# GELU as tanh inside the state-space units of a Hymba-style block, with the mixing stage reading its result directly

## The chip, the cores and the metric

The kernel runs on one core of a Trainium2 chip. The metric is the device time of one execution in microseconds (us). The core has a matrix engine (TensorE, PE; its weight loads are listed apart as PEld), an elementwise engine (VectorE, DVE), an engine for functions and copies (ScalarE, ACT), a slower general engine (GpSimd, POOL) and a queue engine that issues most DMAs (SyncE, SP). Each engine runs its own instructions in order; between engines they wait on semaphores.

## The reference

One layer of a streaming encoder, sequence 2048, model width 1024, all in float32. A normalised input is projected into two head groups. Group A is a state-space layer (32 channel groups of 16, a diagonal complex state of 64 per group), group B chunked attention (8 heads of 64, 64-frame chunks, 8 chunks back, relative-position bias). Both outputs are normalised, joined, projected and added to the input, and a SwiGLU feed-forward follows. The part that the change touches:

```python
def s5_mixer(u, ..., d_skip, w_glu, b_glu):
    ...
    _, states = lax.associative_scan(combine, (a, bu), axis=1)
    y = jnp.einsum('bsgp,ghp->bsgh', states, c_mat).real + d_skip * uf
    y = jax.nn.gelu(y.reshape(bsz, seq, D_SSM))
    y = y * jax.nn.sigmoid(y @ w_glu + b_glu)
    return y
```

`jax.nn.gelu` is here the tanh form, 0.5 y (1 + tanh(sqrt(2/pi) (y + 0.044715 y^3))).

## The kernel before

Matrix products that need float32 accuracy are made from three float32r products: an operand is split into a high part (a cast on ACT) and a low part (a subtraction on DVE). `split` (L151) does both, and `mm3` (L145) the three products.

Time runs in four stages. Up to about 130 us the input of the state-space layer is projected and its matrices are prepared. Then comes **attention** with 128 steps (4 blocks of 512 positions, 8 heads, 4 query tiles of 128 each), up to about 725 us. After it the **mixing stage** (normalisation, sigmoid gate, output projection), up to about 970 us, and the feed-forward.

In an attention step `s` the loop at the end of `att_phase` puts out, in this order of ORDER = "sptf": the scores of step `s` (`sc`, PE; the biased minimum `mn`, DVE; `exp`, ACT, L865), the transposes of step `s - 2` (`pt`, PE, L877; the cast `pth`, ACT, L880; the difference `ptl`, DVE, L881), products with V every four steps (`pj`; `yt` on ACT, `ya` on DVE), and filler. The banks `sc` and `pt` exist once, `pj` twice. PE's instructions keep the order of the program (`Ordered`, PINA), the other engines' instructions are placed by a scheduler, in an order that is then fixed.

Filler is a list of `Unit`s. Each is a generator with a number of pieces, a first step `s0` and an end step `s1`; its first piece may come `pre` steps earlier. Projections of later blocks (`hT_unit`, `qk_unit`, `v_unit`) are units, and so is the state-space layer: eight batches `b` of four channel groups, each with a front and a back.

- `ssm_front(b)` loads `U` (the input, for even `b` from 2 on in the space of `rsn`) and the input matrices, multiplies (`pj`), copies the result to `X` (ACT, L578), and runs the scan over `X` on POOL (L592 to L604). POOL then sends `X`, shifted by one, by four DMAs into `XG` (L626). `X`, `XG` and the odd `U` exist once.
- `ssm_back(b)` loads its two matrices, and in two halves `q` multiplies `U` and `XG` into `pj` and copies it back over `U` (ACT, L648). Eight DMAs on SP store `U` as `y` (L651).

The fronts begin at the steps in SX and last 9 steps, the backs begin at those in SY and last 2.

`mix_phase` works on the four blocks of 512 positions. `fetch` (L1030) loads `y` for two blocks into the tile `yr`, in the order j, c of the state-space layer (position = 8 c + j). `load` applies GELU on ACT, in blocks 0 and 1 by one instruction of 128x2048, in 2 and 3 by four of 128x512, and writes `ys` in order of position; then it splits `ys` into `gh`, `gl`. `load_a` loads the attention outputs `ya` and squares and sums them (`squares`). `glu` multiplies `gh`, `gl` by the gate matrix, adds the bias, takes the sigmoid and multiplies `ys` by it. In blocks 0 and 1 (`late`) the four biased products are put down in `yr`, and one sigmoid of 128x2048 follows; in 2 and 3 each product has its own sigmoid into `sg`. Sums of squares go through PE and a chain of 15 small DVE instructions (`newton`, ending in `no`). The first pieces of `mix_phase`, up to the gates of blocks 0 and 1, are laid into the last attention steps, from step OPEN = 119 on, and the load of the gate matrix (`wgh`, `wgl`, through two buffers `sg`) with them.

Of the kernel before, what the change touches and what calls it, by code (L numbers as in the profile page):

```python
# [16 lines left out]
P = 128  # L17
# [5 lines left out]
L = 8  # L23
# [30 lines left out]
X1B = 6  # L54
TAIL = (0, 512), (512, 256), (768, 256)
MAGIC = 12582912.0
F2 = NF // 2
SB_, CB_, GB_ = 5, 5, 10
DG = 3
# [91 lines left out]
def split(k, hi, lo, raw):  # L151
    nc = k.nc
    return nc.scalar.copy(hi, raw), nc.vector.tensor_tensor(lo, raw, f32(hi), op=ALU.subtract)  # L153
# [400 lines left out]
def ssm_front(k, p, psum, S, b, eng):  # L554

    nc = k.nc

    def load(out, in_):
        ins = nc.sync.dma_start(out, in_)
        if b == 0:  # L560
            k.tc.keep_in_program_order(ins)

    U = S["rsn"][:, : GB * NC].rearrange("p (g c) -> p g c", g=GB) if b and b % 2 == 0 else k.t(p, "U", [P, GB, NC])[:]
    k.U[b] = U
    for j in range(L):
        load(U[j * CH : (j + 1) * CH].rearrange("c g (n t) -> c g n t", n=NSB), S["u"].rearrange("(c g) n j t -> c g n j t", c=CH)[:, GB * b : GB * b + GB, :, j])
    bst = k.t(p, "Bst", [P, GB, P])
    load(bst[:].rearrange("p g m -> p (g m)"), S["bst"][b // 2][:, (b % 2) * GB * P : (b % 2 + 1) * GB * P])
    yield

    X = k.t(p, "X", [P, 2, GP, NC])
    for q in range(GP):
        ps = k.t(psum, "pj", [P, 2, NC], bufs=2)
        for g2 in range(2):
            k.ta.matmul(ps[:, g2, :], bst[:, 2 * q + g2, :], U[:, 2 * q + g2, :], start=True, stop=True)
        for g2 in range(2):
            for c in range(2):
                nc.scalar.copy(X[g2 * NS : (g2 + 1) * NS, c, q, :], ps[c * NS : (c + 1) * NS, g2, :])  # L578
        yield

    a8 = S["a8"]
    qs = slice(GP * b, GP * b + GP)
    Xk = X[:].rearrange("p r q (k s) -> p r q k s", s=8)
    Xe = Xk[:, :, :, :, 7].rearrange("p r q (a b) -> p r q a b", b=8)

    def step(dst, src, e, n):

        ar = a8[:, 0, qs, (0, 7, 15)[e]].unsqueeze(1).to_broadcast([P, 2, GP]).unsqueeze(3).to_broadcast([P, 2, GP, n])
        aw = S["sw"][:, e, :, qs].unsqueeze(3).to_broadcast([P, 2, GP, n])
        t = k.t(p, "st1", [P, 2, GP, NC // 8])  # L590
        t2 = k.t(p, "st2", [P, 2, GP, NC // 8])
        eng.tensor_tensor(t[:, :, :, :n], src, ar, op=ALU.mult)  # L592
        eng.tensor_tensor(t2[:, :, :, :n], src[:, ::-1], aw, op=ALU.mult)
        eng.tensor_tensor(dst, dst, t[:, :, :, :n], op=ALU.add)  # L594
        eng.tensor_tensor(dst, dst, t2[:, :, :, :n], op=ALU.add)  # L595

    def carry(dst, end, i0, n):

        for c in range(2):
            for e in range(2):  # L600
                t = k.t(p, "fx", [P, GP, NC // 8, 7])[:, :, :n]
                pw = a8[:, c if e == 0 else 1 - c, qs, i0 : i0 + 7].unsqueeze(2).to_broadcast([P, GP, n, 7])
                eng.tensor_tensor(t, end[:, e].unsqueeze(3).to_broadcast([P, GP, n, 7]), pw, op=ALU.mult)  # L603
                eng.tensor_tensor(dst[:, c], dst[:, c], t, op=ALU.subtract if e == 1 and c == 0 else ALU.add)  # L604
            yield

    for s in range(1, 8):
        step(Xk[:, :, :, :, s], Xk[:, :, :, :, s - 1], 0, NC // 8)
        yield
    for b_ in range(1, 8):  # L610
        step(Xe[:, :, :, :, b_], Xe[:, :, :, :, b_ - 1], 1, 4)
        yield
    for a in range(1, 4):
        step(Xe[:, :, :, a : a + 1, 7], Xe[:, :, :, a - 1 : a, 7], 2, 1)
        yield
    yield from carry(Xe[:, :, :, 1:, :7], Xe[:, :, :, :3, 7], 8, 3)
    yield from carry(Xk[:, :, :, 1:, :7], Xk[:, :, :, : NC // 8 - 1, 7], 0, NC // 8 - 1)

    if b == 0:
        k.XG = k.t(p, "XG", [P, GB, NC])  # L620
        nc.gpsimd.memset(k.XG[:, :, 0:1], 0.0)
    XG = k.XG
    XGv = XG[:].rearrange("p (q g) c -> p q g c", g=2)
    for g2 in range(2):
        for c in range(2):
            eng.dma_start(XGv[c * NS : (c + 1) * NS, :, g2, 1:], X[g2 * NS : (g2 + 1) * NS, c, :, : NC - 1])  # L626
    yield


def ssm_back(k, p, psum, S, b):  # L630

    nc = k.nc
    F = GB * CH
    gs = slice(GB * b, GB * b + GB)
    tm = k.t(p, "Tm", [P, GB, P])
    for i in range(L):
        nc.sync.dma_start(tm[i * CH : (i + 1) * CH], S["kt"].rearrange("c g a m -> c g (a m)")[:, gs, P - CH * i : 2 * P - CH * i])
    vm = k.t(p, "Vm", [P, GB, P])
    nc.sync.dma_start(vm[:], S["v"].rearrange("q g c n m -> (c n) (q g) m")[:, gs, CH:])
    yield  # L640
    U, XG = k.U.pop(b), k.XG
    for q in range(GP):
        ps = k.t(psum, "pj", [P, 2, NC], bufs=2)
        for g2 in range(2):
            g = 2 * q + g2
            k.ta.matmul(ps[:, g2, :], tm[:, g, :], U[:, g, :], start=True, stop=False)
            k.ta.matmul(ps[:, g2, :], vm[:, g, :], XG[:, g, :], start=False, stop=True)
        nc.scalar.copy(U[:, 2 * q : 2 * q + 2, :], ps[:])  # L648
        yield
    for j in range(L):  # L650
        nc.sync.dma_start(S["y"][b * F : (b + 1) * F, j, :].rearrange("(g c) t -> c g t", c=CH), U[j * CH : (j + 1) * CH])  # L651
    yield


SSM_F = 1 + GP + 7 + 7 + 3 + 4 + 1
SSM_B = 1 + GP + 1
SX = 4, 24, 35, 48, 61, 74, 87, 100
SY = 20, 36, 49, 62, 75, 88, 101, 114


class Unit:
# [21 lines left out]
def att_phase(k, ident, S, aw, x0, roots):  # L683

    tc, nc, io, pfs = k.tc, k.nc, k.io, k.pfs
    with ExitStack() as cx:
# [263 lines left out]
        k.U = {}  # L950
        for b in range(NG // GB):
            units.append(Unit(ssm_front(k, sp, psum, S, b, k.ssm_eng), SSM_F, SX[b], SX[b] + 9, SX[b] - 2 if b == 0 else 2 if b == 1 else 5, light=SL))
            units.append(Unit(ssm_back(k, sp, psum, S, b), SSM_B, SY[b], SY[b] + 2, 6, light=SL))
        N = len(steps)
        for s in range(N + LAG + 2):
            if s == OPEN:
# [24 lines left out]
def mix_phase(k, S, bank):  # L981
# [3 lines left out]
    with ExitStack() as cx:  # L985
# [46 lines left out]
            for f in range(4):  # L1032
                nc.sync.dma_start(yrs[0][:, f], S["y"][f * P : (f + 1) * P, :, sb * 64 : sb * 64 + 128])

        def load(sb, one=False):
            b = B()
            b.o = {}
            yt = k.t(my, "ys", [P, 4, SB], bufs=2)
            b.ys, b.g = [yt[:, f] for f in range(4)], []
            if sb and sb % 2 == 0:  # L1040
                fetch(sb)
            yv = b.yr = yrs[0][:, :, :, (sb % 2) * 64 : (sb % 2 + 1) * 64]
            fs = [slice(0, 4)] if one else [slice(f, f + 1) for f in range(4)]
            for s in fs:
                nc.scalar.activation(yt[:, s].rearrange("p f (c j) -> p f c j", j=L), yv[:, s].rearrange("p f j c -> p f c j"), AF.Gelu_apprx_tanh)
            for f in range(4):
                gh, gl = k.t(my, f"gh{f}", [P, SB], F32R), k.t(my, f"gl{f}", [P, SB], F32R)
                split(k, gh[:], gl[:], b.ys[f])
                b.g.append((gh, gl))
            return b  # L1050

# [5 lines left out]

        def glu(b, bank, late=False):


            def by8(a):
                return a.rearrange("p (a b) -> p a b", a=L)

            for f in range(4):
                ps = bank()
                cs = slice(f * P, (f + 1) * P)
                for q in range(4):
                    mm3(te, ps[:, :512], Wg[q][0][:, cs], Wg[q][1][:, cs], b.g[q][0][:], b.g[q][1][:], q == 0, q == 3)
                    if q < 3:
                        yield  # L1070
                if late:
                    nc.vector.tensor_scalar(b.yr[:, f], by8(ps[:, :512]), bg[:, f : f + 1], None, op0=ALU.add)
                    if f == 3:
                        nc.scalar.activation(b.yr, b.yr, AF.Sigmoid)
                        for i in range(4):
                            nc.vector.tensor_tensor(by8(b.ys[i]), by8(b.ys[i]), b.yr[:, i], op=ALU.mult)
                else:
                    sg = k.t(mz, "sg", [P, SB], bufs=SGB)
                    nc.scalar.activation(sg[:], ps[:, :512], AF.Sigmoid, bias=bg[:, f : f + 1])
                    nc.vector.tensor_tensor(b.ys[f], b.ys[f], sg[:], op=ALU.mult)  # L1080
                yield
            b.sqs = squares(b.ys)

# [73 lines left out]
        yield  # L1157
        mw = rx.enter_context(tc.tile_pool(name="mw", reuse_waits="tile", bufs=2, side="right"))
        wr = rx.enter_context(tc.tile_pool(name="wr", reuse_waits="tile", bufs=2, side="right"))
        b = load(0, True)  # L1160
        load_a(b, 0)
        raws = [load_wo(n, wr, "xt") for n in range(2)]
        for _ in range(PY):
# [1 line left out]
        for n, _ in enumerate(glu(b, bank, True)):  # L1165
# [4 lines left out]
                spread(k, te, pb, b.o[0], 0)  # L1170
                rstd2(b, 0, pb[:])
            yield
        nxt = load(1, True)
        for _ in range(PZ):
            yield

# [551 lines left out]
```

## Time and profile before

| | us |
|---|---|
| median of 3 runs | 2274.19 |
| lowest, highest | 2266.21, 2277.7 |
| the profiled execution | 2277.4 |
| its span in the trace | 2275.6 |

Busy in that span: PE 2169.8 us, DVE 1542.7, ACT 1002.5, POOL 350.1; mean granted clock of PE 0.978. ACT has 15 loads of a function table, 1283 ns each.

A line of a group names the source line, engine, operation, output and inputs with shapes and the count; then busy us and the mean ns of one; then the engine's idle time just before these instructions and what ended it. A line of the timeline begins with the start and the duration in us; the bracket at its end is the idle time of the engine before it and what released it. A line of waits gives the engine and the tile it wrote, what it waited for, the total in us, the number of times and the longest. A line by stretches gives the stretch, its length, the busy time of PE, PEld, DVE, ACT and POOL with counts, the granted clock, and the share and rate of the DMA engines. L153 is the line in `split`, L76 and L79 are PE's products and transposes, `SPq` and `POOLq` are queues that issue DMAs.

### The profile page before, as it was taken

What the parts mean: (1) busy time and instruction counts of PE and PEld (TensorE: products, weight loads), DVE (VectorE), ACT (ScalarE), POOL (GpSimd) and SP (SyncE); (2) the same over time, 40 slices, a digit from 0 to 9 for tenths busy, and PEclk for the clock granted to TensorE, in tenths of its full rate; (3) what the DMA queues carried; (4) which work ended last, traced back from release to release, by engine and by line L of the source; (5) the groups of instructions that cost most, each with busy time, mean ns of one, the idle gap of its engine ahead of it and who ended that gap; (6) DMA issues with size and microseconds to landing.
All of it is one profiled execution on the core that took longest, in us unless ns stands there. A gap on an engine that the chain in (4) does not pass through costs nothing.

```text
span 2275.6 us, 30307 instructions
## 1 busy us (share of the span) xinstructions
PE 2169.8 (95%) x10632; PEld 1828.5 (80%) x10632; DVE 1542.7 (68%) x2695; ACT 1002.5 (44%) x1656; POOL 350.1 (15%) x827
## 2 busy tenths in 40 slices
PE   8989898999997899999999999999999999999997
PEld 6778787888986688878888887888888777888886
DVE  7757556555556756776767678666666477688776
ACT  6446555455557452343333335333333443353322
POOL 2246666646520000000000000000000010000000
PEclk9999999999998899999999999999999999999999
DMA  8778875766653535854555467655433395465652
GB/s 296 234 250 263 220 195 172 220 197 185 177 166 105 172 118 160 270 179 144 178 183 193 163 213 259 196 175 185 143 93 115 110 389 169 166 226 182 218 179 75
DMA packets 214874, 428.36 MB, mean 188 GB/s; under 512 B 38848, under 2 KB 61424, under 8 KB 207616
## 3 DMA queue, kind: packets, MB, share of 16 engines
q1 hardware_dynamic: 207072, 401.49, 54.6%
q0 software_dynamic: 7648, 24.92, 3.3%
q8 instruction: 84, 1.38, 0.2%
q14 instruction: 70, 0.57, 0.1%
HBM read 286.86 MB, written 129.00 MB: 183 GB/s over the span
## 4 chain that ended last, share of the span: by engine, by line
PE 77%; DMA 5%; DVE 5%; issue 4%; POOL 3%; ACT 2%; SPq 1%; DVEq 0%; ACTq 0%; POOLq 0%
PE X L76 20%; PE ps L76 17%; PE Y L76 10%; PE big L76 9%; PE pf L76 8%; PE W L76 5%; PE pj L76 3%; PE sc L76 2%; DMA acc<-x 2%; PE pt L79 2%; POOL X L595 1%; POOL X L594 1%; DMA lo<-hc 1%; POOL X L604 1%; POOL fx L603 1%
## 5 line engine op out<-in xcount | busy, mean ns | idle before, releaser
L76 PE MATMUL X<-hi,c 128*128 128x512 f32 x1408 | 451.3, 391 | 6.2 <-DVE c L153 5.5
L76 PE MATMUL ps<-hd,hd 128*128 128x512 f32 (+1 forms) x1968 | 429.7, 380 | 3.9 <-DVE hd L153 2.0
L76 PEld LDWEIGHTS ps<-hd,hd 128*128 128x128 f32 x1968 | 357.6, 189 | 74.6 <-DVE hd L153 2.7
L76 PEld LDWEIGHTS X<-hi,c 128*128 128x128 f32 x1408 | 265.4, 189 | 62.7 <-DVE c L153 6.4
L76 PE MATMUL X<-lo,c 128*128 128x512 f32 x704 | 274.9, 390 | 0.0
L153 ACT CAST hd<-hd 128x1536 fp32r<-128x1536 f32 (+1 forms) x106 | 147.3, 1393 | 234.6 <-DMA hd<-hq 148.1
L76 PE MATMUL Y<-hi,c 128*128 128x512 f32 x704 | 224.7, 390 | 2.1 <-DVE u L1407 2.1
L153 DVE TENSOR_TENSOR hd<-hd 128x1536 fp32r<-128x1536 f32 (+1 forms) x106 | 174.0, 1643 | 37.1 <-ACT hd L153 36.5
L153 DVE TENSOR_TENSOR c<-S,c 128x512 fp32r<-128x512 f32 x176 | 120.8, 687 | 98.9 <-ACT c L153 98.7
L1511 POOL DMA_DIRECT2D hd<-hq x7 | 5.3, 762 | 1169.5 <-PE X L76 1158.0
L1403 ACT COPY u<-X 128x512 f32<-128x512 f32 x132 | 77.3, 586 | 200.6 <-PE X L76 200.6
L76 PE MATMUL big<-m,woh 128*128 128x512 f32 x512 | 163.1, 400 | 0.0
L153 ACT CAST c<-S 128x512 fp32r<-128x512 f32 x176 | 109.3, 621 | 119.0 <-PE Y L76 61.8
L1545 DVE TENSOR_TENSOR acc<-acc,ps 128x512 f32<-128x512 f32 x196 | 130.3, 681 | 41.0 <-PE ps L76 40.7
L76 PEld LDWEIGHTS Y<-hi,c 128*128 128x128 f32 x704 | 132.3, 188 | 30.4 <-DVE u L1407 2.9
L76 PEld LDWEIGHTS X<-lo,c 128*128 128x128 f32 x704 | 132.8, 189 | 27.7
L76 PE MATMUL pf<-hi,w 128*128 128x512 f32 x416 | 150.7, 414 | 0.8 <-ACT hi L741 0.8
L153 ACT CAST c<-raw 128x512 fp32r<-128x512 f32 x132 | 82.2, 622 | 151.0 <-PE Y L76 64.3
L881 DVE TENSOR_TENSOR ptl<-pt,pth 128x640 fp32r<-128x640 f32 (+3 forms) x152 | 98.2, 646 | 66.6 <-ACT pth L880 64.8
L76 PE MATMUL Y<-lo,c 128*128 128x512 f32 x352 | 137.0, 389 | 0.0
L865 ACT ACTIVATE s<-s,mn 128x640 f32<-128x640 f32 (+4 forms) x128 | 97.9, 765 | 74.1 <-DVE mn L862 67.1
L880 ACT CAST pth<-pt 128x640 fp32r<-128x640 f32 (+3 forms) x152 | 83.6, 550 | 82.6 <-PE pt L79 77.6
(448 smaller groups left out, 4280.6 us busy)
## 6 DMA issues: line engine op xcount, KB each, us to landing
w<-wss SPq DMA_DIRECT2D x36, 1024.0 KB, 6.6
hq<-g SPq DMA_DIRECT2D x140, 256.0 KB, 2.1
hd<-hq SPq DMA_DIRECT2D x35, 768.0 KB, 4.5
hd<-wc SPq DMA_DIRECT2D x35, 768.0 KB, 5.9
raw<-in_w_gate SPq DMA_DIRECT2D x44, 512.0 KB, 3.7
raw<-in_w_up SPq DMA_DIRECT2D x44, 512.0 KB, 4.2
wc<-px SPq DMA_DIRECT2D x66, 256.0 KB, 2.9
wss<-w SPq DMA_DIRECT2D x12, 1024.0 KB, 5.8
```

Source lines behind the costliest of these rows:

```text
L76: return self.tc.keep_in_program_order(self.tc.nc.tensor.matmul(*a, **b))
L79: return self.tc.keep_in_program_order(self.tc.nc.tensor.transpose(*a, **b))
L153: return nc.scalar.copy(hi, raw), nc.vector.tensor_tensor(lo, raw, f32(hi), op=ALU.subtract)
L594: eng.tensor_tensor(dst, dst, t[:, :, :, :n], op=ALU.add)
L595: eng.tensor_tensor(dst, dst, t2[:, :, :, :n], op=ALU.add)
L603: eng.tensor_tensor(t, end[:, e].unsqueeze(3).to_broadcast([P, GP, n, 7]), pw, op=ALU.mult)
L604: eng.tensor_tensor(dst[:, c], dst[:, c], t, op=ALU.subtract if e == 1 and c == 0 else ALU.add)
L865: nc.scalar.activation(s[:, :nk], s[:, :nk], AF.Exp, bias=mn[:], scale=-1.0, accum_out=sums[sb, pr][:, hh, qp : qp + 1])
L880: nc.scalar.copy(pth[:, a:b, qp, :], pt[:, a:b, :])
L881: nc.vector.tensor_tensor(ptl[:, a:b, qp, :], pt[:, a:b, :], f32(pth[:, a:b, qp, :]), op=ALU.subtract)
L1403: nc.scalar.copy(u[:], ps[:])
L1545: V.tensor_tensor(a, a, ps[:], op=ALU.add)
```

## The change

Each half of a back now leaves 0.5 y in `U` (ACT copy with a scale), its square in the same half of `XG`, then on DVE (square + 0.25/0.044715) times 0.5 y, tanh on ACT with the remaining factor as its scale, and on DVE (tanh + 1) times 0.5 y over `U`. A back has 8 pieces in place of 4 and takes 4 steps; from the fourth batch on fronts start every 12 steps instead of 13, and from the third on backs come earlier (the last at step 108 instead of 114). Since `XG` is overwritten, POOL clears its first column for each batch. `load` no longer calls GELU: the splits read `yr` itself, its rows j in steps of 128 elements, and write `gh` and `gl` in order of position. The late sigmoid works in `ys`, and the final product multiplies the sigmoid by `yr`, again read across its rows.

```diff
     if b == 0:
         k.XG = k.t(p, "XG", [P, GB, NC])
-        nc.gpsimd.memset(k.XG[:, :, 0:1], 0.0)
     XG = k.XG
+    nc.gpsimd.memset(XG[:, :, 0:1], 0.0)
...
-        nc.scalar.copy(U[:, 2 * q : 2 * q + 2, :], ps[:])
+        u, t = U[:, 2 * q : 2 * q + 2, :], XG[:, 2 * q : 2 * q + 2, :]
+        nc.scalar.activation(u, ps[:], AF.Copy, scale=0.5)
+        nc.scalar.activation(t, u, AF.Square)
+        yield
+    for q in range(GP):
+        u, t = ...
+        nc.vector.scalar_tensor_tensor(t, t, 0.25 / GELU, u, op0=ALU.add, op1=ALU.mult)
+        nc.scalar.activation(t, t, AF.Tanh, scale=8.0 * GELU * math.sqrt(2.0 / math.pi))
+        yield
+    for q in range(GP):
+        u, t = ...
+        nc.vector.scalar_tensor_tensor(u, t, 1.0, u, op0=ALU.add, op1=ALU.mult)
         yield
...
-SSM_B = 1 + GP + 1
-SX = 4, 24, 35, 48, 61, 74, 87, 100
-SY = 20, 36, 49, 62, 75, 88, 101, 114
+SSM_B = 1 + 3 * GP + 1
+SX = 4, 24, 35, 47, 59, 71, 83, 95
+SY = 20, 36, 48, 60, 72, 84, 96, 108
...
-            units.append(Unit(ssm_back(k, sp, psum, S, b), SSM_B, SY[b], SY[b] + 2, 6, light=SL))
+            units.append(Unit(ssm_back(k, sp, psum, S, b), SSM_B, SY[b], SY[b] + 4, 6, light=SL))
...
-            for s in fs:
-                nc.scalar.activation(yt[:, s].rearrange("p f (c j) -> p f c j", j=L), yv[:, s].rearrange("p f j c -> p f c j"), AF.Gelu_apprx_tanh)
+            b.yr = yrs[0][:, :, :, (sb % 2) * 64 : (sb % 2 + 1) * 64].rearrange("p f j c -> p f c j")
             for f in range(4):
-                split(k, gh[:], gl[:], b.ys[f])
+                split(k, byt(gh[:]), byt(gl[:]), b.yr[:, f])
...
                 if late:
-                    nc.vector.tensor_scalar(b.yr[:, f], by8(ps[:, :512]), bg[:, f : f + 1], None, op0=ALU.add)
+                    nc.vector.tensor_scalar(b.ys[f], ps[:, :512], bg[:, f : f + 1], None, op0=ALU.add)
                     if f == 3:
-                        nc.scalar.activation(b.yr, b.yr, AF.Sigmoid)
+                        nc.scalar.activation(b.yt[:], b.yt[:], AF.Sigmoid)
                         for i in range(4):
-                            nc.vector.tensor_tensor(by8(b.ys[i]), by8(b.ys[i]), b.yr[:, i], op=ALU.mult)
+                            nc.vector.tensor_tensor(byt(b.ys[i]), byt(b.ys[i]), b.yr[:, i], op=ALU.mult)
                 else:
-                    nc.vector.tensor_tensor(b.ys[f], b.ys[f], sg[:], op=ALU.mult)
+                    nc.vector.tensor_tensor(byt(b.ys[f]), byt(sg[:]), b.yr[:, f], op=ALU.mult)
```

The order that each engine gets is fixed when the kernel is built. ACT near the end of attention, before, from a head's `exp` (`s`) to the casts of block 0 for the gate; `pth` is the cast of the transposes, `yt` the copy behind the products with V:

```order
L865 ACTIVATE s_8141,sm_8105<-s_8141,mn_8142 128x640
L1045 ACT_TABLE_LOAD
L1045 ACTIVATE ys_8185<-yr_8069 128x2048
L153 CAST wgh_1709_8074<-sg_8076 128x512
L153 CAST wgh_1712_8080<-sg_8082 128x512
L904 COPY yt_8166<-pj_8149 64x512
L880 CAST pth_8169<-pt_8171 128x5x128
L153 CAST gh_1741_8187<-ys_8185 128x512
L153 CAST gh_1743_8191<-ys_8185 128x512
L153 CAST gh_1745_8195<-ys_8185 128x512
L153 CAST gh_1747_8199<-ys_8185 128x512
```

The same place now (source lines are 12 higher in this part):

```order
L154 CAST gh_1741_8257<-yr_8140 128x512
L877 ACTIVATE s_8192,sm_8176<-s_8192,mn_8193 128x640
L892 CAST pth_8087<-pt_8196 128x5x128
L154 CAST gh_1743_8261<-yr_8140 128x512
L877 ACTIVATE s_8212,sm_8176<-s_8212,mn_8213 128x640
L154 CAST gh_1745_8265<-yr_8140 128x512
L154 CAST gh_1747_8269<-yr_8140 128x512
L154 CAST wgh_1709_8145<-sg_8147 128x512
L154 CAST wgh_1712_8151<-sg_8153 128x512
L916 COPY yt_8237<-pj_8220 64x512
L892 CAST pth_8240<-pt_8242 128x5x128
```

The load and the GELU are gone, and the four casts have moved ahead of the `yt` and `pth` behind which they stood. In the whole order of ACT 3 table loads are left of 15.

SP at the same place, before: loads of the gate matrix through `sg`, and of the attention outputs of block 0 (`ya_1749` to `ya_1752`):

```order
L1000 DMA sg_8082<-in_w_glu 128x512
L549 DMA nbb_1549<-nbs_69 64x576
L550 DMA nbb_1549<-nbs_69 64x576
L1055 DMA ya_1749_8203<-ya_s_66 128x512
L1055 DMA ya_1750_8204<-ya_s_66 128x512
L1055 DMA ya_1751_8205<-ya_s_66 128x512
L1055 DMA ya_1752_8206<-ya_s_66 128x512
L1000 DMA sg_8088<-in_w_glu 128x512
L1000 DMA sg_8094<-in_w_glu 128x512
```

SP now:

```order
L1012 DMA sg_8153<-in_w_glu 128x512
L550 DMA nbb_1549<-nbs_69 64x576
L551 DMA nbb_1549<-nbs_69 64x576
L1067 DMA ya_1749_8273<-ya_s_66 128x512
L1012 DMA sg_8159<-in_w_glu 128x512
L1012 DMA sg_8165<-in_w_glu 128x512
L1067 DMA ya_1750_8274<-ya_s_66 128x512
L1067 DMA ya_1751_8275<-ya_s_66 128x512
L1067 DMA ya_1752_8276<-ya_s_66 128x512
```

Three of the four `ya` loads have moved behind the second pair of loads of the gate matrix, which need the `sg` buffers free again.

DVE in the last back, now: the four three-operand products (`XG`, `U`) among the minimum of the scores (`mn`) and the `ptl` of attention; before, none of the four was there:

```order
L800 TENSOR_TENSOR k_1588_7439<-pf_7521,k_1588_7439 64x512
L655 SCALAR_TENSOR_TENSOR XG_2225<-XG_2225,U_6701 128x512
L874 ISA s_7659,mn_7660<-sc_7654,nbb_1549 128x640
L874 ISA mn_7660 128x1
L660 SCALAR_TENSOR_TENSOR U_6701<-XG_2225,U_6701 128x512
L655 SCALAR_TENSOR_TENSOR XG_2225<-XG_2225,U_6701 128x512
L893 TENSOR_TENSOR ptl_7561<-pt_7663,pth_7560 128x5x128
L660 SCALAR_TENSOR_TENSOR U_6701<-XG_2225,U_6701 128x512
```

Each `U` product stands ahead of the next softmax instruction of DVE and needs a Tanh of ACT first.

More of the change, by code (lines that the diff above doesn't have):

```diff
@@ L56 @@
 MAGIC = 12582912.0
+GELU = 0.044715
 F2 = NF // 2
@@ L647, in ssm_back @@
             k.ta.matmul(ps[:, g2, :], vm[:, g, :], XG[:, g, :], start=False, stop=True)
-        nc.scalar.copy(U[:, 2 * q : 2 * q + 2, :], ps[:])
+        u, t = U[:, 2 * q : 2 * q + 2, :], XG[:, 2 * q : 2 * q + 2, :]
[3 more added lines that the diff above has]
+    for q in range(GP):
+        u, t = U[:, 2 * q : 2 * q + 2, :], XG[:, 2 * q : 2 * q + 2, :]
+        nc.vector.scalar_tensor_tensor(t, t, 0.25 / GELU, u, op0=ALU.add, op1=ALU.mult)
+        nc.scalar.activation(t, t, AF.Tanh, scale=8.0 * GELU * math.sqrt(2.0 / math.pi))
+        yield
+    for q in range(GP):
+        u, t = U[:, 2 * q : 2 * q + 2, :], XG[:, 2 * q : 2 * q + 2, :]
+        nc.vector.scalar_tensor_tensor(u, t, 1.0, u, op0=ALU.add, op1=ALU.mult)
         yield
@@ L1033, in fetch, with byt, load @@
                 nc.sync.dma_start(yrs[0][:, f], S["y"][f * P : (f + 1) * P, :, sb * 64 : sb * 64 + 128])
-        def load(sb, one=False):
+        def byt(a):
+            return a.rearrange("p (c j) -> p c j", j=L)
+        def load(sb):
             b = B()
             b.o = {}
-            yt = k.t(my, "ys", [P, 4, SB], bufs=2)
-            b.ys, b.g = [yt[:, f] for f in range(4)], []
+            b.yt = k.t(my, "ys", [P, 4, SB], bufs=2)
+            b.ys, b.g = [b.yt[:, f] for f in range(4)], []
             if sb and sb % 2 == 0:
                 fetch(sb)
-            yv = b.yr = yrs[0][:, :, :, (sb % 2) * 64 : (sb % 2 + 1) * 64]
-            fs = [slice(0, 4)] if one else [slice(f, f + 1) for f in range(4)]
-            for s in fs:
-                nc.scalar.activation(yt[:, s].rearrange("p f (c j) -> p f c j", j=L), yv[:, s].rearrange("p f j c -> p f c j"), AF.Gelu_apprx_tanh)
+            b.yr = yrs[0][:, :, :, (sb % 2) * 64 : (sb % 2 + 1) * 64].rearrange("p f j c -> p f c j")
             for f in range(4):
                 gh, gl = k.t(my, f"gh{f}", [P, SB], F32R), k.t(my, f"gl{f}", [P, SB], F32R)
-                split(k, gh[:], gl[:], b.ys[f])
+                split(k, byt(gh[:]), byt(gl[:]), b.yr[:, f])
                 b.g.append((gh, gl))
@@ L1058, in glu @@
         def glu(b, bank, late=False):
-            def by8(a):
-                return a.rearrange("p (a b) -> p a b", a=L)
             for f in range(4):
@@ L1159, in mix_phase @@
         wr = rx.enter_context(tc.tile_pool(name="wr", reuse_waits="tile", bufs=2, side="right"))
-        b = load(0, True)
+        b = load(0)
         load_a(b, 0)
@@ L1172, in mix_phase @@
             yield
-        nxt = load(1, True)
+        nxt = load(1)
         for _ in range(PZ):
```

## The prediction

> **What bounds the kernel now.** I read the page's engine totals first, then TensorE's list of waits over the whole span, then busy time by stretches, and last the order of time between 684 and 760 us.
>
> ```profile
> PE 2169.8 (95%) x10632; PEld 1828.5 (80%) x10632; DVE 1542.7 (68%) x2695; ACT 1002.5 (44%) x1656; POOL 350.1 (15%) x827
> PE pt L79 <- DVE ptl L881: 17.9, 8, 6.1
> PE sc L76 <- DVE mn L862: 9.9, 5, 3.8
> PE big L79 <- DVE no L110: 7.8, 1, 7.8
> PE pf L76 <- DVE lo L742: 3.6, 1, 3.6
> 600.00:660.00 60.00, 60.00 (x392) 55.64 (x391) 33.03 (x60) 33.42 (x65) 34.72 (x88) 1.00 0.51 144
> 690.00:730.00 40.00, 26.82 (x136) 22.58 (x137) 26.61 (x55) 31.21 (x44) 0.00 (x0) 0.79 0.22 73
> 730.00:760.00 30.00, 22.18 (x101) 17.67 (x101) 29.53 (x54) 22.77 (x30) 0.00 (x0) 0.88 0.61 210
> 760.00:820.00 60.00, 59.74 (x262) 49.36 (x261) 32.91 (x72) 32.81 (x41) 0.00 (x0) 0.94 0.34 110
> ```
>
> TensorE (PE) is busy 95% of the span, so only time in which PE waits, or runs at a lower granted clock, can be won. The columns of the stretches are PE, weight loads, VectorE (DVE), ScalarE (ACT) and GpSimd (POOL) busy, then the clock. Attention (600 to 660) fills PE, with DVE and ACT little over half busy. From 760 on, the mixing stage fills it too. Between them, at the end of attention, PE idles 13.2 of 40 us and then 7.8 of 30, at clocks of 0.79 and 0.88. In the first of these ACT is the busiest engine (31.2 of 40), in the second DVE (29.5 of 30). In time:
>
> ```profile
> 686.88 1.28 ACT L1045 ACT_TABLE_LOAD   x1
> 688.17 3.72 ACT L1045 ACTIVATE ys<-yr 128x2048 f32<-128x2048 f32 x1
> 693.54 0.69 ACT L880 CAST pth<-pt 128x640 fp32r<-128x640 f32 x1
> 698.42 1.28 ACT L865 ACT_TABLE_LOAD   x1
> 699.72 0.83 ACT L865 ACTIVATE s<-s,mn 128x640 f32<-128x640 f32 x1
> 701.58 0.67 ACT L880 CAST pth<-pt 128x640 fp32r<-128x640 f32 x1
> 703.08 1.28 ACT L1045 ACT_TABLE_LOAD   x1
> 704.37 3.79 ACT L1045 ACTIVATE ys<-yr 128x2048 f32<-128x2048 f32 x1
> 695.44 1.30 PE L79 MATMUL pt<-ident,s 128*128 128x128 f32 x5 [6.14 <-DVE ptl L881]
> 703.56 1.30 PE L79 MATMUL pt<-ident,s 128*128 128x128 f32 x5 [5.75 <-DVE ptl L881]
> 709.65 0.77 PE L79 MATMUL pt<-ident,s 128*128 128x128 f32 x5 [1.16 <-DVE ptl L881]
> ```
>
> The transposes `pt` have one bank, so each waits until the previous one was cast (`pth`, ACT) and subtracted (`ptl`, DVE). The casts at 693.54 and 701.58, and the one after the second GELU, stand in ACT's queue behind a table load and a GELU of 3.7 us. That is PE's 6.14 + 5.75 + 1.16 = 13.05 us.
>
> **The change part by part.** *GELU leaves the mixing stage.* The order of ACT falls from 15 table loads to 3; the 12 that go cost 12 x 1.28 = 15.4 us of ACT, and 7.5 + 8.7 us of GELU go too:
>
> ```profile
> L1045 ACT ACTIVATE ys<-yr 128x512 f32<-128x512 f32 x8 | 8.7, 1125 | 2.3 <-DVE m L153 2.3
> L153 ACT CAST gh<-ys 128x512 fp32r<-128x512 f32 x16 | 9.0, 616 | 1.7 <-PE pf L76 1.6
> 684.18 1.82 SPq L1055 DMA_DIRECT2D ya<-ya_s  x4
> 693.15 0.94 SPq L1000 DMA_DIRECT2D sg<-in_w_glu  x2
> ya<-ya_s SPq DMA_DIRECT2D x8, 256.0 KB, 5.1
> sg<-in_w_glu SPq DMA_DIRECT2D x4, 256.0 KB, 4.1
> ```
>
> The 16 casts `gh` now read `yr` across its rows, as GELU did, so each rises from 0.616 to about 1.125 us (GELU's row for the same access): +8.1 us on ACT, 2.0 of it in each block. From 760 on none of this is worth anything, since PE idles 0.26 of 60 us there. At the end of attention the gain is less than PE's 13.05 us, because of what is late next. In the new order of ACT the four casts stand where load and GELU stood (4.5 us against 1.28 + 3.72), two of them ahead of `exp` and `pth`. So the 693.54 cast comes only about 1.8 us earlier (691.7), and its PE transposes start near 693.7. Then SP's order, shown above, decides: three of the four `ya` loads, issued from 684.18 on before, now stand behind the second pair of `w_glu` loads, which waits for DVE to release `sg` (693.15; about 1 us earlier now). Issued near 693 to 694, they land 5.1 us later, at about 698.5. ACT's square of the second `ya` stands ahead of the next `pth`, so this cast runs near 699 (701.58 before) and the second PE wait ends near 700.5 instead of 703.56: 3 us. The load and GELU at 703.08 (5.07 us) are gone, so the third wait goes as well, and PE, with 4.5 us of its own work between, arrives near 705 at what began at 709.65. Term one: **-5 us**; bounds 0 and -13 (all three waits). Of the lower clock I count nothing: long waits remain, and after a wait the matmuls are slow as before (the five transposes took 1.30 us at 695 and 0.77 at 709).
>
> By the Trainium skill (ScalarE: Activation LUTs, What ACT_TABLE_LOAD costs) a switch costs 1.28 us and about 1.38 us of drain. Here the load is 1.28 us and the work behind it starts 0.01 us later (688.17), so the trace shows no drain; with it, four switches would be worth 5.5 us more.
>
> *Splits and final products read `yr` strided on DVE.* The nearest DVE rows are one product with unit steps and one whose operands step by 32 bytes:
>
> ```profile
> L483 DVE TENSOR_TENSOR us<-ps,pb x8: 676/678/693, 44.3 to 93.9; 128x512 f32<-128x512 f32 x8
> L483 DVE TENSOR_TENSOR us<-ps,rsn x4: 1114/1120/1166, 115.0 to 118.1; 128x512 f32<-128x512 f32 x4
> 731.69 2.50 DVE L1076 TENSOR_TENSOR ys<-ys,yr 128x512 f32<-128x512 f32 x4
> 736.14 0.68 DVE L914 TENSOR_TENSOR ya<-ya,pj 128x512 f32<-128x512 f32 x1
> 736.85 0.32 SPq L915 DMA_DIRECT2D ya_s<-ya  x1
> 737.21 1.88 SPq L1005 DMA_DIRECT2D m<-in_w_out  x4
> ```
>
> So +0.44 us for each of 32 instructions if 512-byte steps (no row has them on DVE) cost what 32-byte steps do, 0 if they cost nothing. I take 0.44, since ACT, whose rows have such steps, nearly doubles. Sixteen lie in 760 to 960, under a full PE: 0. Four lie near 690 beside ACT's casts. Twelve lie in 725 to 757, where DVE is never free: the second block's `gl`, the first block's `ys` product, the second's. The first eight (3.5 us) run ahead of `ya` at 736.14; its store heads SP's queue, and the `w_out` loads behind it (737.21) feed ACT's casts, the second sigmoid, and, in DVE's order, the Newton steps that end PE's 7.75 us wait for `no`. The last four stand between those steps. Term two: 12 x 0.44 = **+5.3 us**; bounds 0 and 5.3.
>
> The Trainium skill (SBUF — State Buffer, Door 1: The DMA port swizzle) speaks against the change here: lines are 16 bytes, and an access pays when it crosses to a new one, which 32 and 512 bytes both do at each fp32 element. By that rule the term is +5.3; with unit-step prices it would be 0.
>
> *GELU in the state-space units.* Eight units, two halves each: the evacuation stays one copy (0.587 us, now with a scale), and each half adds a Square and a Tanh on ACT and two three-operand products on DVE, beside POOL's scan:
>
> ```profile
> L648 ACT COPY U<-pj 128x512 f32<-128x512 f32 x10 | 5.8, 587 | 12.1 <-PE pj L76 10.8 <-DMA Bst<-bsts 1.4
> L1021 ACT ACTIVATE sg<-ya 128x512 f32<-128x512 f32 x12 | 7.3, 627 | 4.7 <-DVE sq L1022 4.7
> L740 DVE SCALAR_TENSOR_TENSOR raw<-raw,g_mix,rsn 128x512 f32<-128x512 f32 x12 | 11.1, 955 | 3.0 <-DMA raw<-in_xt 3.0
> L1093 DVE SCALAR_TENSOR_TENSOR ys<-ys,gs,big 128x512 f32<-128x512 f32 x16 | 11.0, 741 | 0.0
> L865 ACT ACTIVATE s<-s,mn x128: 399/832/838, 137.3 to 720.9; 128x640 f32<-128x640 f32 x96, 128x128 f32<-128x128 f32 x8, 128x256 f32<-128x256 f32 x8, 128x384 f32<-128x384 f32 x8
> ```
>
> ACT +16 x 2 x 0.627 = 20 us; DVE +16 x 2 x 0.955 = 30.6 us (24 at the price without POOL). A unit adds 2.5 us of ACT and 3.8 of DVE over four steps of 4.6 us (583.6 us for 127 steps); in 600 to 660 both engines have 27 us free in 60. By throughput PE covers it all. By order it doesn't: Tanh waits on ACT for the DVE product, with `exp` or `pth` behind it, and the last product waits on DVE for Tanh, with `mn` or `ptl` behind. Each half can hold the softmax for 0.955 + 0.627 = 1.6 us. PE feels that only where `sc` or `pt` (one bank each) come due in it; uncovered it is 16 x 1.6 = 25 us. It can also win: the unit's matmuls move by up to six steps, and the waits for `lo` (3.6) and one for `mn` (3.8) may lose their cause: -7. I take a quarter of the uncovered cost, since PE has a step's slack: term three **+6 us**; bounds -7 and +25. The stores of `y` on SP, with the `w` and `k` loads behind them, wait for the last product; they are issued two steps ahead of use, so 0. POOL's seven added memsets (0.1 us) wait for the unit before, which ends some five steps earlier: 0.
>
> Sum: -5 + 5.3 + 6 = **+6 us**. The profiled execution took 2277.4 us, so 2283.4 for one like it; the median shown is 3.2 lower at 2274.2, so I predict **2280 us**. Its own range: term one -8 to -3, two 3.5 to 5.3, three 0 to 10, so 2274.7 to 2286.5, say 2272 to 2287.
>
> **Rivals.** *Softmax held by the new chain (slower).* At ACT and DVE in the four steps of each unit: if 11 of 16 halves hit PE, three is +17.6 and the sum +18: 2292; all of them 2299. It decides once `mn` or `ptl` are over two steps late. For: PE already waits for `mn` and `ptl` in attention. Against: the full PE at 600 to 660, which has a unit's copies in it.
>
> *The end of attention pays in full (faster).* If the `ya` loads land early, all 13.05 us go, the clock rises from 0.79 to 0.94 (26.82 us of PE become 22.5: 4.3 more), half of the strided cost is covered and the units cost nothing: -17.4 + 2.6 = -15, 2259. For: ACT sheds four loads and two GELUs there, 12.6 us. Against: SP's order.
>
> *POOL's ring is too tight (slower).*
>
> ```profile
> 290.51 3.02 ACT L578 COPY X<-pj 64x256 f32<-64x256 f32 x8 [7.73 <-DMA XG<-X]
> 332.29 1.21 POOL L626 DMA_DIRECT2D XG<-X  x2 [0.30 <-POOL X L604]
> XG<-X POOLq DMA_DIRECT2D x32, 127.5 KB, 5.0
> ```
>
> The copies of a unit wait until the unit before has sent `X` away: 333.5 + 5 - 290.5 = 48 us. Twelve steps are 55 us on average, thirteen were 60. It decides where steps fall under 4 us; 2 us at each of five units: +10 more, 2290.
>
> *With the drain.* The skill's 1.38 us per switch would make it 5.5 us less: 2274.5.
>
> **How the numbers follow.** Forecast 0.50, softmax held 0.28, paid in full 0.14, POOL's ring 0.04, drain 0.04. A measurement here can tell about 0.5%, 11.4 us. Faster by more (under 2262.8): half of the paid-in-full case and a little of the forecast's edge, 0.09. Slower by more (over 2285.6): most of the softmax case (0.25), half of the ring's (0.02), the forecast's upper edge (0.05), 0.32. Within: 0.59. For 8 in 10 the range reaches 2262 to 2297: outside lie the lower half of one rival and the upper third of the other, and a few hundredths at the forecast's own unknowns.
>
> **What would show it.** Right: 3 table loads; PE waits for `ptl` between 690 and 730 that shrink to about 8 us but stay; `gl` and `ys` products near 1.1 us and PE's wait for `no` nearer 13 us; new waits of 1 to 2 us for `mn` or `ptl` near the units. Wrong: `gl` at 0.69 us; no wait for `ptl` at the end of attention; waits for `X`; PE's idle time in 130 to 690 unchanged.

## The result, and the profile after

The changed kernel takes 2293.27 us (median of 6 runs, 2291.42 to 2295.41) against 2274.01 us before (6 runs, 2266.21 to 2277.7). The ratio is 1.008, with a 95% interval of 1.0066 to 1.0094: 15 to 21 us slower. The profiled execution took 2291.4 us, with a span of 2289.6 us. Below, "+x us" of a kernel is its ratio less one, times 2274.

The totals of the page come first, then TensorE's list of waits over the whole span (time in all, times, longest), then busy time by stretches (columns as in the prediction):

```profile
PE 2169.8 (95%) x10632; PEld 1829.5 (80%) x10632; DVE 1576.2 (69%) x2727; ACT 996.4 (44%) x1666; POOL 365.1 (16%) x834
PE pf L77 <- DMA w<-wss: 21.1, 5, 10.4
PE pt L80 <- DVE ptl L893: 11.3, 8, 3.6
PE pj L77 <- DMA U<-u: 8.5, 1, 8.5
PE big L80 <- DVE no L111: 7.8, 1, 7.8
130.00:690.00 560.00, 503.84 (x3031) 450.32 (x3032) 329.30 (x619) 306.84 (x652) 311.74 (x728) 0.96 0.66 198
700.00:740.00 40.00, 32.31 (x175) 27.05 (x174) 31.42 (x61) 26.77 (x44) 0.00 (x0) 0.89 0.35 113
```

PE does the same 2169.8 us of work as before, so the added time is idle time. The end of attention got better: in its 40 us PE idles 7.7 us (13.2 before), and the waits for `ptl` fall from 17.9 to 11.3 us over the span. What is new stands at the top of the list. PE waits 21.1 us for weight pairs `w`, a wait that before did not have, and 8.5 us for `U`, at matmuls that waited 4.2 us before. Both lie in the body of attention. There PE idles 56 us between 130 and 690 us; in the kernel before it idled 43:

```profile
130.00:690.00 560.00, 516.74 (x3113) 462.84 (x3113) 320.33 (x609) 305.12 (x643) 299.46 (x725) 0.96 0.70 205
```

The two longest waits for `w`, and lines of SP's queue ahead of each (start, duration, instruction; others are left out):

```profile
343.71 0.79 PE L77 MATMUL pf<-w,hi0x 128*128 128x256 f32 x2 [10.41 <-DMA w<-wss]
328.70 0.58 SPq L638 DMA_DIRECT2D Tm<-kts  x1
329.80 4.90 SPq L560 DMA_DIRECT2D U<-u  x8
335.25 0.94 SPq L719 DMA_DIRECT2D w<-wss  x2
582.51 0.80 PE L77 MATMUL pf<-w,hi0x 128*128 128x256 f32 x2 [7.83 <-DMA w<-wss]
564.84 2.45 SPq L638 DMA_DIRECT2D Tm<-kts  x5
567.81 4.00 SPq L560 DMA_DIRECT2D U<-u  x8
572.81 1.56 SPq L719 DMA_DIRECT2D w<-wss  x2
```

The same two places in SP's queue before, again without the lines between:

```profile
312.12 0.58 SPq L707 DMA_DIRECT2D w<-wss  x1
317.30 0.54 SPq L707 DMA_DIRECT2D w<-wss  x1
324.46 4.47 SPq L637 DMA_DIRECT2D Tm<-kts  x8
538.34 0.53 SPq L707 DMA_DIRECT2D w<-wss  x1
560.97 0.44 SPq L707 DMA_DIRECT2D w<-wss  x1
562.61 7.81 SPq L637 DMA_DIRECT2D Tm<-kts  x8
```

Counted from the first, the two loads at 335.25 are those at 312.12 and 317.30 before, and the two at 572.81 are those at 538.34 and 560.97. Before, they are issued ahead of the unit's `Tm`, `Vm` and `U`; after, behind them, 12 to 34 us later. PE was ready at 343.71 - 10.41 = 333.3, before the pair was even issued. By the `exp` of the same step, the kernel after is 4.9 us behind the kernel before at step 44 and 16.4 us at step 48, with the first of these waits between them; at the second it goes from 6.6 us (step 92) to 19.4 (step 96). So the closer starts of the units reached SP's queue, which the prediction followed only past the stores of `y`.

### The profile page after: what moved, and what is told of

The parts are those of the page before. It is cut to its first block, busy times and chain, and to the rows that moved or that the text cites. A ratio compares the mean times of both kernels' runs of the same rounds, so it can differ in the third digit from the quotient of the medians.

```text
span 2289.6 us, 30340 instructions
## 1 busy us (share of the span) xinstructions
PE 2169.8 (95%) x10632; PEld 1829.5 (80%) x10632; DVE 1576.2 (69%) x2727; ACT 996.4 (44%) x1666; POOL 365.1 (16%) x834
## 4 chain that ended last, share of the span: by engine, by line
PE 77%; DMA 6%; DVE 6%; issue 3%; ACT 2%; POOL 2%; SPq 1%; DVEq 0%; ACTq 0%; POOLq 0%
PE X L77 21%; PE ps L77 17%; PE Y L77 10%; PE pf L77 8%; PE big L77 8%; PE W L77 5%; PE pj L77 3%; PE sc L77 2%; PE pt L80 2%; DMA acc<-x 2%; DMA w<-wss 1%; DVE ptl L893 1%; DVE s L874 1%; DMA yr<-x 0%; DVE ys L1084 0%
## 5 line engine op out<-in xcount | busy, mean ns | idle before, releaser
L1415 DVE TENSOR_TENSOR u<-u,Y 128x512 f32<-128x512 f32 x88 | 60.4, 686 | 80.5 <-ACT u L1411 60.6
```

The costliest lines, as they stand in the source:

```text
L1415: V.tensor_tensor(u[:], u[:], ps[:], op=ALU.add)
```

## The experiments

Each was timed beside the kernel before. Their names are used below. Two accounts stand against each other: the *queue theory* (the moved loads hold the weight pairs in SP's queue) and the *chain theory* (GELU's instructions on ACT and DVE hold the softmax).

**e1, the closer starts alone.** The kernel before with one table changed:

```diff
-SX = 4, 24, 35, 48, 61, 74, 87, 100
-SY = 20, 36, 49, 62, 75, 88, 101, 114
+SX = 4, 24, 35, 47, 59, 71, 83, 95
+SY = 20, 36, 48, 60, 72, 84, 96, 108
```

Expected:

> The kernel before with only the closer starts of the units (the new starting steps of fronts and backs); GELU stays at the load of the mixing stage. Queue theory (the earlier steps put the loads of Tm, Vm and U ahead of weight pairs w in SP's in-order queue, and PE waits for those pairs; the trace of after shows 10.4 + 1.1 + 7.8 = 19.4 us of such waits that before does not have): about +19 us, 2288 to 2295, with PE waits for w near 340 and 580 us. Chain theory (the GELU arithmetic on ACT and DVE holds the softmax): no change, 2271 to 2278.

Measured: 2289.18 us, ratio 1.0068 (1.0052 to 1.0083), +15.5 us. PE's waits of e1 between 130 and 690 us:

```profile
PE pf L76 <- DMA w<-wss: 20.8, 5, 8.0
```

With no GELU in the units at all, the waits for `w` are there, and the time is the queue theory's. The table of starts alone costs most of what the change costs.

**e2, the old starts with everything else of the change.** The inverse edit, on the kernel after. Expected:

> The kernel after with the old starting steps of the units; GELU in the units and the mixing stage as changed. Queue theory: the 19.4 us of waits for w go, 2270 to 2278. Chain theory: the arithmetic is all there, so it stays at 2289 to 2297.

Measured: 2287.45 us, 1.007 (1.0049 to 1.009), +15.9 us. This is a miss for the queue theory, and 1.6 us under the chain theory's range:

```profile
PE sc L77 <- DVE mn L874: 9.6, 4, 4.0
PE pt L80 <- DVE ptl L893: 9.3, 9, 2.4
PE pf L77 <- DMA w<-wss: 4.7, 2, 3.0
```

The waits for `w` do shrink from 21.1 to 4.7 us, but those for `ptl` and `mn` are large (5.4 and 1.1 in the kernel after in the same stretch), and the 8.5 us for `U` stays. The waits for `mn` belong to the old starts, not to GELU: the kernel before has 9.9 us of them. Its waits for `ptl` are 4.9 us, 4.4 less than here. So GELU in the units has a price of its own, which depends on where the units stand.

**e3, only the loads moved back.** The kernel after, computing at the same steps, with the units' loads issued later:

```diff
-    ... SX[b] - 2 if b == 0 else 2 if b == 1 else 5, light=SL))
-    ... SY[b], SY[b] + 4, 6, light=SL))
+    ... SX[b] - 2 if b == 0 else 2 if b == 1 else 3 if b == 7 else 4, light=SL))
+    ... SY[b], SY[b] + 4, 4 if b == 6 else 5, light=SL))
```

> The kernel after, its computing at the same steps, but the backs issue their loads 5 steps ahead instead of 6 (4 for the seventh) and the fronts 4 instead of 5 (3 for the eighth), so that these loads stand behind the weight pairs in SP's queue again. Queue theory: the waits for w go, about 19 us less than after, 2270 to 2278. Chain theory: 2290 to 2296 as after. A third possibility: Tm or U now come late in their turn, with PE waits for Tm or U of a few us, 2278 to 2288.

Measured: 2279.56 us, 1.0023 (1.0009 to 1.0036), +5.2 us, which is 13.0 us less than the kernel after. It lies 1.6 us above the queue theory's range, in that of the third possibility (loads that now come late): PE's wait for `U` is 10.1 us here, 8.5 in the kernel after. No work was taken away, only a place in a queue:

```profile
PE pf L77 <- DMA w<-wss: 6.9, 3, 4.8
```

The waits for `w` fell by 14 us, from 21.1, and the time by 13. What is left of them, and the wait for `U`, is taken up in e7.

**e4, GELU left out, the loads where the change put them.** Each half only copies its product out; the steps of the window stay.

> The kernel after with the GELU left out of the state-space layer (each half only copies its product out; the steps that held GELU's work stay empty), the new starts and the mixing stage as after. Queue theory: the Tm, Vm and U loads still stand ahead of both weight pairs, so 2283 to 2293, the stores of y a little earlier. Chain theory: the whole loss in attention goes, 2266 to 2274.

Measured: 2286.83 us, 1.0057 (1.0041 to 1.0074), +13.0 us. The chain theory alone falls: without GELU, two thirds of the loss are still there.

**e5, the mixing stage alone.** Units and starts as before, GELU left out altogether:

> The kernel after with the state-space units of before (one copy out per half, old window, old starts) and the GELU left out of the kernel altogether; only the change of the mixing stage remains: strided splits and products, no GELU loads, one sigmoid over four tiles. Sum of the prediction's terms one and two: -5 + 5.3, so 2274 (2272 to 2277). By the trace of after, whose lag against before falls by 7.5 us at the last softmax steps and rises by 4.2 us until no: 2271 (2268 to 2273).

Measured: 2272.99 us, 0.9994 (0.9981 to 1.0008), -1.4 us (-4 to +2). The prediction's first two terms cancel, as they did there. The interval holds the gain of 3.3 us read from the trace of after (7.5 less 4.2) as well.

**e6, GELU left out, the loads moved back (e3 with e4).**

> The kernel of the third experiment (loads behind the weight pairs) with GELU left out of the units: each half only copies its product out, the steps that held GELU stay empty. Its difference from the third experiment is the price of the arithmetic. Chain theory: all that is left goes, 2268 to 2272 (7 to 11 us less). Queue theory: what is left is the store of y at the end of a long window, with U and w behind it, which stays: 2275 to 2280 (0 to 4 us less).

Measured: 2269.76 us, 0.9982 (0.9968 to 0.9996), -4.1 us. It gives, with e3 and e4, a table of two edits (us against before):

| | GELU in the units | GELU left out | price of GELU |
|---|---|---|---|
| loads ahead of `w` (after, e4) | +18.2 | +13.0 | 5 |
| loads behind `w` (e3, e6) | +5.2 | -4.1 | 9 |
| price of the loads' place | 13 | 17 | |

Each price is uncertain by 4 to 5 us. The closer starts, once their loads are out of the way of `w`, cost nothing (e6 is 2.7 us under e5, which has the old starts). e6 itself came out as the chain theory had it: without GELU all that was left went, though its wait for `U` (9.4 us) stayed. So neither theory holds alone: the place of the loads is the larger part, the arithmetic the smaller. In PE's lists the largest part of GELU's price is again the wait for `w`, 4.0 us more in the kernel after than in e4 and 5.4 more in e3 than in e6; the waits for `ptl`, of transposes and products together, are 3.3 and 0.4 us more.

**e7, the first two units' backs in 2 steps instead of 4** (on e3).

> The kernel of the third experiment, but the backs of the first two units run in 2 steps as before instead of 4, GELU in them. Queue theory: y of the first unit leaves earlier, U of the second unit, which takes the same tile, lands earlier, PE's 8.7 us wait for U falls to about 4 to 5: 2273 to 2277. Chain theory: the same arithmetic twice as dense holds the softmax more, 2280 to 2285.

Measured: 2273.74 us, 1.0001 (0.9987 to 1.0016): 5 us less than e3, uncertain by 4 to 5. PE's wait for the second unit's `U` was 8.73 us in e3; here, at the same matmuls, the wait is the 3.60 us that the list puts down to the load of `k` (in the kernel before 4.20, put down to the store of `k`). In order: before, e3 with its SP queue, e7 with its SP queue:

```profile
240.77 3.75 PE L76 MATMUL pj<-U,Bst 128*128 128x256 f32 x8 [4.20 <-DMA ks<-k]
245.74 3.75 PE L77 MATMUL pj<-U,Bst 128*128 128x256 f32 x8 [8.73 <-DMA U<-u]
226.53 1.81 SPq L663 DMA_DIRECT2D y<-U  x2
232.53 1.06 SPq L802 DMA_DIRECT2D ks<-k  x2
233.64 2.81 SPq L663 DMA_DIRECT2D y<-U  x6
238.25 3.89 SPq L560 DMA_DIRECT2D U<-u  x8
241.17 3.75 PE L77 MATMUL pj<-U,Bst 128*128 128x256 f32 x8 [3.60 <-DMA k<-ks]
227.98 3.86 SPq L663 DMA_DIRECT2D y<-U  x8
234.30 3.99 SPq L560 DMA_DIRECT2D U<-u  x8
```

The second unit's `U` is the first unit's tile, so its loads wait until `y` has been read out of it. GELU's last product is not what holds them: in e3 it ends at 226.24, before the first store is issued. With the window of four steps six of the eight stores stand behind two stores of `k`, which wait for DVE until 232.53; with two steps all eight go in one run from 227.98, ahead of them. So this wait too is a place in SP's queue. e6, without GELU in the same window, has the same order there and the wait too.

**e8, the stores of `y` issued by POOL** (on e3).

```diff
-        nc.sync.dma_start(S["y"][b * F : (b + 1) * F, j, :]...
+        nc.gpsimd.dma_start(S["y"][b * F : (b + 1) * F, j, :]...
```

> The kernel of the third experiment with the stores of y issued by POOL instead of SP, so that no load of SP's queue stands behind a store that waits for GELU's last product. Queue theory: the 6.9 us of PE waits for w go, the wait for U stays or shrinks: 2268 to 2276. Against it: POOL's own queue now waits for that product and its scan of the next unit starts later, PE waits for X: 2280 to 2290.

Measured: 2319.58 us, 1.0203 (1.0181 to 1.0224), +46 us, worse than both expectations. PE's wait, SP's own, and the last product of the second unit with the stores behind it:

```profile
PE pf L77 <- DMA w<-wss: 27.8, 4, 14.6
SPq L560 <- DMA y<-U: 61.3, 6, 18.8
309.12 0.88 DVE L660 SCALAR_TENSOR_TENSOR U<-XG,U 128x512 f32<-128x512 f32 x1
335.82 4.10 POOL L663 DMA_DIRECT2D y<-U  x8
```

Moving the stores off the queue did not free it. The loads of `U` on SP must wait for those stores, now on POOL, which issues them late: in six of the eight units 25 to 28 us after the last product, behind the scan of the next unit (0.03 us in e3). `w` stands behind `U`. PE waited for `w`, not for `X` as the rival had it (3.1 us, 3.0 in e3).

**e9, all eight backs in 2 steps** (on e3), and **e10, the old starts with backs in 2 steps**:

> The kernel of the third experiment with the backs of all eight units in 2 steps instead of 4, GELU in them. Window theory (what the arithmetic still costs is the late end of a long window: y, then U and w, leave late): a little below the seventh experiment, 2270 to 2274. Throughput theory (ACT and DVE hold the softmax while they do the arithmetic, the more the denser): 2276 to 2282.

> The kernel after with the old starts of the units (second experiment) and the backs in 2 steps as before, so that only GELU and the mixing stage differ from before. Window theory: the second experiment's U wait (8.5 us against 4.2) and w waits (4.7) go, 9 us less, 2274 to 2279. Throughput theory: 2284 to 2292.

Measured: e9 2274.99 us, 0.9998 (0.9981 to 1.0015), no difference from before and none from e7, between the two theories' ranges; e10 2285.24 us, 1.0045 (1.0033 to 1.0058), +10.2 us, where the throughput theory had it. e10 differs from e5 in GELU alone and is 11.6 us slower. PE's waits for `ptl` in e10 (those for `w` are 4.3 us), and one of them in time:

```profile
PE pt L80 <- DVE ptl L893: 10.1, 9, 3.1
490.47 0.71 PE L80 MATMUL pt<-ident,s 128*128 128x128 f32 x5
491.10 0.98 DVE L655 SCALAR_TENSOR_TENSOR XG<-XG,rsn 128x512 f32<-128x512 f32 x1
492.11 0.63 ACT L656 ACTIVATE XG<-XG 128x512 f32<-128x512 f32 x1 [1.43 <-DVE XG L655]
493.98 0.67 ACT L892 CAST pth<-pt 128x640 fp32r<-128x640 f32 x1
495.27 0.75 DVE L752 SCALAR_TENSOR_TENSOR raw<-raw,g_mix,rsn 128x512 f32<-128x512 f32 x1 [0.73 <-DMA raw<-in_xt]
495.94 0.82 DVE L893 TENSOR_TENSOR ptl<-pt,pth 128x640 fp32r<-128x640 f32 x1
496.81 0.76 PE L80 MATMUL pt<-ident,s 128*128 128x128 f32 x5 [3.09 <-DVE ptl L893]
```

The transposes end at 491.18, but `pth` is cast only from 493.98 on: ahead of it in ACT's order stand GELU's Tanh, which first waits 1.43 us for its product on DVE, a Square and an `exp`. Then DVE takes `ptl` only at 495.94, behind a scaling whose load came late, and PE waits 3.09 us. In e5 the same list shows 3.1 us for `ptl` in all and none for `w`. e10's 11.6 us are not GELU's instructions alone: 41 of its 406 DMAs on SP between 200 and 690 us stand out of e5's order. Why GELU costs 12 us at the old starts and 4 at the new ones with short windows (e9 less e6) is not settled; the example shows only one such meeting.

**e11, e9 with `w` asked for a step earlier.**

> The kernel of the ninth experiment with the weight pairs of the later q, k and v units asked for 3 steps ahead instead of 2, against the 3.8 us wait for w that the seventh still shows near 338. Queue theory: 2 to 4 us below the ninth, 2266 to 2272, below before. Against it: three w tiles are all there are, so an earlier place in the queue only waits for the tile, and holds what is behind it: the same or up to 5 us more.

Measured: 2274.9 us, 1.0007 (0.9994 to 1.002). The long wait for `w` falls from 5.43 to 2.82 us, but the time does not move clear of noise, as the rival had it. No version here beats the kernel before while doing the same work.

**e12, e10 without GELU's two products on DVE.**

> The kernel of the tenth experiment (old starts, backs in 2 steps) with GELU's two products on DVE left out: ACT still does the scaled copy, the Square and the Tanh of each half (20 us in all). If the price of the arithmetic in the tenth (2285.2 against 2273.0 in the fifth) is ACT's time in front of exp and pth: 2282 to 2286. If it is the products on DVE in front of ptl and mn, and the hops between the two engines: 2272 to 2277.

Measured: 2275.14 us, 0.9997 (0.9987 to 1.0008), 11 us under e10. PE's waits for `ptl` fall back:

```profile
PE pt L80 <- DVE ptl L890: 4.5, 6, 1.4
```

ACT's 20 us of Square and Tanh, without the products, cost nothing that can be told. What carries the price goes with the products, but it is not taken apart: their time on DVE, the hops between the engines, or SP's order, which falls back too (4 of 414 DMAs out of e5's order) and takes the 4.3 us of waits for `w` with it.

## Why the prediction was right in its range and wrong in its size

The point, 2280, was 13 us low; 2293.27 lies inside the whole range (2262 to 2297) but outside the forecast's own (2272 to 2287). That the whole range holds it is luck: it reached so high for the softmax rival, which did not come, and no rival had the mechanism that did. The lower end of its own range was also added up wrongly: -8 + 3.5 + 0 from 2274.2 is 2269.7, not 2274.7. By its steps:

*Term one, GELU out of the end of attention: right.* PE's waits for `ptl` from 690 on were 17.9 - 4.9 = 13.0 us and are 11.3 - 5.4 = 5.9 (about 8 forecast). That is 7 us against the 5 taken, inside the bounds. Two waits stayed, behind what the working named: the casts in ACT's order, and the `w_glu` cast that waits 1.56 us for its load. The page has the three table loads that were forecast.

*Term two, strided reads on DVE: right.* The groups of DVE and ACT from 690 us on:

```profile
L154 DVE TENSOR_TENSOR gl<-yr,gh 128x512 fp32r<-128x512 f32 x16 | 16.8, 1092 | 0.7 <-ACT gh L154 0.7
L1084 DVE TENSOR_TENSOR ys<-ys,yr 128x512 f32<-128x512 f32 x8 | 8.2, 1063 | 0.0
L154 ACT CAST gh<-yr 128x512 fp32r<-128x512 f32 x16 | 17.5, 1116 | 2.3 <-PE pf L77 1.1 <-DMA yr<-y 1.1
```

`gl` and `ys` take 1.09 and 1.06 us (0.684 and 0.685 before), so 512-byte steps do cost what 32-byte steps did: +0.4. The casts `gh` rose from 0.616 to 1.116, as forecast. The rule of the Trainium skill that spoke against the change here (SBUF — State Buffer, Door 1: The DMA port swizzle: each access that crosses to a new 16-byte line pays) agrees with these rows. From the second block's first `gl` to `no`, DVE's order takes 32.3 us against 28.0 before, +4.2 (5.3 forecast). PE's wait for `no` did not grow to 13 us: it is 7.8, with a new 3.0 us wait for `ya` ahead of it, at 750.27. In e5 the two are 9.5 and 3.0, 12.4 together. Terms one and two together are e5's -1.4; the prediction had +0.3.

*Term three, the units: this is the step that failed.* It said +6, bounds -7 and +25; measured is after less e5, 18.2 + 1.4 = 19.6 us. It has two parts. The first sentence to fail is "The stores of `y` on SP, with the `w` and `k` loads behind them, wait for the last product; they are issued two steps ahead of use, so 0". It looked at what stands behind the stores, and not at the other instructions of the moved steps: the starts moved the loads of `Tm`, `Vm` and `U` past the weight pairs. That cost 13 us (e3), 15.5 alone (e1), and was counted at nothing. The longer window moved the stores themselves behind those of `k` as well (e7). "The unit's matmuls move" was counted as a possible gain only. The second part is the arithmetic, "a quarter of the uncovered cost", +6: 5 to 9 us at the new starts, 11.6 at the old ones (e10 less e5). That size holds for the kernel as changed, but by luck: of the waits from which it was worked out, those for `mn` fell and those of the transposes for `ptl` rose by 0.5 us, and the largest part of GELU's price shows as waits for `w`. The prediction read attention off 600 to 660 us, where PE never idles; from 130 to 690 PE idled 43 us before the change. The four groups on DVE between 130 and 690 us:

```profile
L655 DVE SCALAR_TENSOR_TENSOR XG<-XG,U 128x512 f32<-128x512 f32 x10 | 8.3, 829 | 6.3 <-ACT XG L651 6.3
L660 DVE SCALAR_TENSOR_TENSOR U<-XG,U 128x512 f32<-128x512 f32 x10 | 7.7, 766 | 0.5 <-ACT XG L656 0.5
L655 DVE SCALAR_TENSOR_TENSOR XG<-XG,rsn 128x512 f32<-128x512 f32 x6 | 5.2, 864 | 4.8 <-ACT XG L651 4.7
L660 DVE SCALAR_TENSOR_TENSOR rsn<-XG,rsn 128x512 f32<-128x512 f32 x6 | 4.6, 769 | 0.0
```

They sum to 25.8 us against the 30.6 forecast: 0.8 us each on average rather than the 0.955 of the row taken.

*The rivals.* "Softmax held by the new chain" gave the time (2292) but by another cause: it put 18 us on `mn` and `ptl`, whose waits in the body of attention are 1.1 and 5.4 us in the kernel after, 9.9 and 4.9 before. "Paid in full" did not come: the waits for `ptl` stay, and the clock of that stretch is 0.89, not 0.94. POOL's ring was not too tight: one wait for `X` of 2.8 us, where before had 4.3 in two. No drain shows: the table load at 739.77 takes 1.28 us, and ACT's next work starts at 741.06.

## What to carry to other kernels

A table of starts moves every instruction that a step issues, its DMAs among them: list which loads each moved load passes on its in-order queue, and when their readers want them. Here 17 loads of two units, wanted five to six steps later, came to stand in front of a weight pair that was wanted next, and that cost more than the 64 new compute instructions. Where a store waits for new arithmetic, follow the tile it reads as well as the queue it stands in: another queue for the store only moved the wait to the next load into that tile (e8).

## What was not expected of the hardware

The same product on DVE takes 0.68 us or up to half as long again. Ten of the sixteen `XG` products of the kernel after (shortest, median, longest ns), and two stretches, that of the first unit's GELU and that of the last one's:

```profile
L655 DVE SCALAR_TENSOR_TENSOR XG<-XG,U x10: 682/752/1046, 217.8 to 654.1; 128x512 f32<-128x512 f32 x10
217.00:225.00 8.00, 7.61 (x40) 6.13 (x39) 6.70 (x15) 6.69 (x16) 0.11 (x1) 1.00 0.82 282
652.00:657.00 5.00, 5.00 (x38) 4.64 (x37) 4.41 (x8) 3.65 (x7) 0.00 (x0) 1.00 0.19 75
```

The shape is one, and both operands lie in SBUF. In the two stretches POOL, the fifth column, does next to nothing, and their eight products (four `XG`, four `U`) all take 0.68 to 0.70 us. The other 24 all overlap an instruction of POOL's scan: 15 of them take over 0.8 us, up to 1.05, and some still 0.68. The Trainium skill (GPSIMD Engine Reference, Specifications) says that POOL shares its SBUF interfaces with VectorE and contends with instructions of two SBUF inputs. The trace agrees: none of the long ones stands where POOL is idle. No run here took POOL's work away to show it by experiment.
